# Retention's tiles from four pools, its roots stored by step, a shorter lag in attention, and row fetches issued five steps sooner

## The chip, the cores and the metric

The kernel runs on one core of a Trainium2 chip. The metric is the device time of one execution in microseconds. Before the change it is 1906.09 us, the median of three runs (1904.04 to 1906.96).

A core has a matrix engine (TensorE, PE in the profile; its weight loads are PEld), three engines for elementwise work (VectorE or DVE, ScalarE or ACT, GpSimd or POOL) and a synchronisation engine (SyncE or SP), which here issues most of the DMA transfers; ScalarE issues the weight streams. Each engine runs its instructions in order. Data lies in the main memory, in SBUF (128 partitions) and in PSUM, where TensorE writes its products.

## The reference

One layer of an encoder over 2048 positions and a model width of 1024, in float32:

```python
h = rms_norm(x, norm_gain)
q_a, k_a, v_a, g_a, q_r, k_r, v_r, g_r, m_a, m_r = split_columns(h @ w_in)
o_a = chunk_band_attention(q_a, k_a, v_a, rel_bias)     # 8 heads of 64, chunks of 64, 8 chunks to the left
branch_a = (o_a * silu(g_a)) @ w_out_attn
o_r = retention_chunkwise(rotary(q_r), rotary(k_r), v_r, gn_gain)   # 8 heads, keys of 64, values of 128
branch_r = (o_r * silu(g_r)) @ w_out_ret
mixed = sigmoid(m_a) * branch_a + sigmoid(m_r) * branch_r
out = rms_norm(x + mixed @ w_out, final_gain)
```

Retention is a product of queries and keys under a decay mask, times the values, plus a state that is carried from step to step. Its output is normalised for each head and position: the mean over the 128 values is taken away, and the rest is multiplied by the reciprocal root of its variance.

## The kernel before, in words

Most products are held to float32 accuracy by splitting an operand into a high and a low part and adding three products. The large projections run as Strassen products over two halves of the sequence (s = 0, 1), of two blocks of 512 positions each (b = 0 to 3).

The stages are p0 (projections of the first half), attention and retention of the first half, p1, attention and retention of the second half, and then the output products (ba, br, out) on 23 buffers. While attention and retention run, TensorE is filled up with products of the next projection: `fill(n)` (line 686) takes n steps of a stream that `dense` (line 627) yields, where a step is a quarter of a product, three matmuls of 512 columns. The order of all instructions on each engine is the order in which the program writes them. Work that has to wait for other work is put off with `later(n, fn)` (line 245): fn is written out n steps on. `put` (line 258) does that with a store.

SBUF tiles come from pools. A pool of n buffers gives a tile a buffer whose earlier tile is done with; the first instruction that writes the new tile waits until the last use of the old one is over, be it an engine's read or a store. `E` (line 114) takes tiles of 128 x 512 from the pool of the phase that is open. Retention's phase has 22 such buffers (`E_RET`, line 57).

Retention (line 1615) handles four pairs of heads (p) and, in each half, four steps of 256 positions (st). A step has two items (i), one for each head of the pair. For an item, `scores` (line 1671) multiplies keys and queries (tile sr in PSUM), VectorE multiplies that by the decay mask (sm<-sr,dm), ScalarE makes the high part (sh), and POOL the low part (sl). `output` (line 1745) multiplies the values by these parts and adds the state's share, in the PSUM bank o, of which there is one. `evacuate` (line 1762) copies o to the tile oz, squares it (o2) on ScalarE, stores oz two steps later (ors<-oz) and splits the squares (o2h, o2l). `sums`, at line 1790, sums the squares over the 128 values with a matmul against a matrix that has a column of ones: the row of the PSUM tile ssq that gets the sum is chosen by which 32 columns of the matrix `ohr` are taken. It uses 32 rows, half of them in each half of the sequence, and 512 columns.

Scores run two items ahead of outputs. The six loads of scored operands (kr<-krs twice, qr<-qrs four times; `load_scored`, line 1624) are issued two steps ahead, those of the values (kd, vr; `load_valued`, line 1646) one step ahead, and a mask (dm; `load_mask`, line 1667) some items ahead of its pair. All of them are written on SP's queue, as are the stores of the gates (mas, mrs) that the stream makes meanwhile.

After the last step of a half a chain of twelve VectorE operations (line 1844) turns ssq into reciprocal roots, and one store writes them to `rsscr` (rss<-rt). `finish_yr` (line 1240) reads a row of them for each head and block, much later. In the first half the loads of a later projection's operands (b_p<-in_w_in, line 1962) are written next.

Attention (line 1413) transposes its weights in groups (tp), splits them (pth on ScalarE, ptl on VectorE), and multiplies the values by them into the PSUM bank po (`weighted`, line 1525). A group's product is put off by `PV_LAG` = 3 slots, that of the first group by 2 more. A slot is one step of filling together with attention's own work. The bank po of the head before is read out (oa<-po) in the meantime. The first group only exists for blocks that have a block to their left.

While p0 runs, `second_half` (line 891) prepares the second half's rows: four pieces, each of four fetches of 128 x 4 x 128 (xs<-in_x), which ScalarE scales eight steps later by the reciprocal norms, TensorE transposes (pst<-ident,xs), and whose sums and differences are stored (cs<-xs, cs<-s).

Of the kernel before, what the change touches and what calls it, by code (L numbers as in the profile page):

```python
# [56 lines left out]
E_RET = 22  # L57
# [12 lines left out]
ONE = 31  # L70
# [3 lines left out]
def hybrid_kernel(  # L74
# [118 lines left out]
    rsscr = [D(f"rss_{s}", [32, B]) for s in range(2)]  # L193
# [697 lines left out]
    def second_half(at):  # L891
# [25 lines left out]
        def piece(k):  # L917
            tiles = {}

            def fetch(i, f):  # L920
                a = tiles[i, f] = E(f"xs_{k}_{i}_{f}", shape=(P, 4, P))
                rows = x[0, (2 + i) * B:(3 + i) * B, 512 * f + k * P:512 * f + (k + 1) * P]
                dma(a, rows.rearrange("(t p) c -> p t c", p=P))
                later(8, lambda: scale(i, f))
# [44 lines left out]
            later(26, first)  # L969
            later(30, second)  # L970
            later(34, third)

        for k in range(4):
            later(at + 14 * 8 + 18 + 44 * k, lambda k=k: piece(k))
# [265 lines left out]
    def finish_yr(h, b, m, lead, hold=0):  # L1240

        a, u, r = (E(f"{n}_{h}_{b}") for n in ("yr", "yv", "rb"))
        dma(a, orscr[h // 2][b][h % 2])
        dma(u, urscr[h][b])
        dma(r, rsscr[b // 2][8 * b + h].rearrange("(o d) -> o d", o=1).broadcast_to([P, B]))

        def gated():
            dve.scalar_tensor_tensor(a, a, gn[:, h:h + 1], u, ALU.mult, ALU.mult)

        later(lead, gated)  # L1250
        later(lead + 2, lambda: (pool if m is None else dve).tensor_tensor(a, a, r, ALU.mult))
        if m is None:
            put(lead + 8, yrscr[h], a)
            return
        wh, wl = (w[:, h % 4, :] for w in R[m])
        at = max(lead + 5, hold - steps[0])
        later(at, lambda: act.copy(wh, a))
        later(at + 2, lambda: dve.tensor_tensor(wl, a, r32(wh), ALU.subtract))
# [154 lines left out]
    def attention(s, sbp, ps_wide):  # L1413
# [111 lines left out]
        def weighted(h, b, gr):  # L1525
# [43 lines left out]
            later(PV_LAG + (2 if gr == 0 else 0), product)  # L1569
# [45 lines left out]
    def retention(s, ps_ret):  # L1615
        RET_FILL = RET_FILLS[s]
        ssq = ps_ret.tile([32, 512], F32, tag="ssq", bufs=1, name="ssq")
# [48 lines left out]

        def load_mask(p, i):
            dms.setdefault(p, []).append(E(f"dm_{p}_{i}")[:, 0:T + P])
            dma(dms[p][i], dmask[2 * p + i])

        def scores(p, st, i):
# [11 lines left out]
            def masked():  # L1683
                sm = E(f"sm_{nm}")[:, 0:T + P]
                dve.tensor_tensor(sm, sp, dms[p][i], ALU.mult)
                later(2, lambda: high(sm))

            def high(sm):
                got.append(E(f"sh_{nm}", F32R)[:, 0:T + P])
# [3 lines left out]
            def low(sm):  # L1693
                got.append(E(f"sl_{nm}", F32R)[:, 0:T + P])
# [67 lines left out]
        def evacuate(p, st, ops):  # L1762
# [4 lines left out]
            def out_():  # L1767
                oz = E(f"oz_{nm}")
                o2 = E(f"o2_{nm}")
# [9 lines left out]
            def high(o2):  # L1779
                got.append(E(f"o2h_{nm}", F32R))  # L1780
# [3 lines left out]
            def low(o2):  # L1784
                got.append(E(f"o2l_{nm}", F32R))
# [4 lines left out]
            def sums():  # L1790
                sure(lambda: len(got) == 2)
                for i in range(2):
                    r = 8 * b + 2 * p + i
                    for n, t in enumerate(got):
                        pe.matmul(
                            ssq[:, un * T:(un + 1) * T], ohr[:, ONE - r:ONE - r + 32],
                            t[:, i * T:(i + 1) * T],
                            start=not begun[0], stop=(p == 3 and st == 4 * s + 3 and i == 1 and n == 1),
                            skip_group_check=True,
                        )  # L1800
                        begun[0] = True
# [41 lines left out]
        y, tmp, hv, var = (E(f"rt{n}")[0:32] for n in range(4))  # L1843
# [11 lines left out]
        chain.append(lambda: dma(rsscr[s], y))  # L1855
# [189 lines left out]
```

## Time and profile before

| | |
|---|---|
| median of three runs | 1906.09 us (1904.04 to 1906.96) |
| profiled execution | 1910.35 us |
| its span, first to last instruction | 1908.5 us |
| TensorE busy | 1866.8 us (98%) |
| VectorE, ScalarE, POOL busy | 1356.3, 932.0, 665.2 us |
| mean granted TensorE clock | 0.996 |
| retention, first half | about 572 to 735 us of the span |
| retention, second half | about 1322 to 1497 us |

Times in the profile are microseconds from the first instruction, unless marked as ns. A row names the engine, the operation, the tiles as output<-inputs (without their buffer numbers), the shapes and how many instructions it stands for. All instructions carry the line of one helper, L143, so tiles are told apart by their names. Brackets behind a row show how long the engine had been idle and what ended that. The granted clock is a share of full speed. TensorE's matmuls overlap, so the time that one costs in a stream is read from start to start.

### The profile page before, as it was taken

What the parts mean: (1) busy time and instruction counts of PE and PEld (TensorE: products, weight loads), DVE (VectorE), ACT (ScalarE), POOL (GpSimd) and SP (SyncE); (2) the same over time, 40 slices, a digit from 0 to 9 for tenths busy, and PEclk for the clock granted to TensorE, in tenths of its full rate; (3) what the DMA queues carried; (4) which work ended last, traced back from release to release, by engine and by line L of the source; (5) the groups of instructions that cost most, each with busy time, mean ns of one, the idle gap of its engine ahead of it and who ended that gap; (6) DMA issues with size and microseconds to landing.
All of it is one profiled execution on the core that took longest, in us unless ns stands there. A gap on an engine that the chain in (4) does not pass through costs nothing. (4 is left out here: it accounts for less than half of the span.)

```text
span 1908.5 us, 31057 instructions
## 1 busy us (share of the span) xinstructions
PE 1866.8 (98%) x10213; PEld 1606.6 (84%) x10213; DVE 1356.3 (71%) x2456; ACT 932.0 (49%) x1931; POOL 665.2 (35%) x583
## 2 busy tenths in 40 slices
PE   7999999999999999999999999999999999999998
PEld 6899889888888877899889888888888878888886
DVE  6879888667655657888798677765546766767665
ACT  7555554666654455443343666664445321223544
POOL 0102105455645552001105545554564000001775
PEclk9999999999999999999999999999999999999999
DMA  6586976666549997776776656545999999987673
GB/s 192 160 273 203 282 266 213 185 181 192 177 133 279 283 264 239 240 233 200 226 246 199 191 155 196 160 150 168 265 278 276 317 354 346 318 294 228 209 235 129
DMA packets 325553, 435.88 MB, mean 228 GB/s; under 512 B 29880, under 2 KB 191184, under 8 KB 325392
## 3 DMA queue, kind: packets, MB, share of 16 engines
q1 hardware_dynamic: 260096, 368.35, 60.3%
q10 hardware_dynamic: 65296, 65.55, 11.3%
q8 instruction: 81, 1.33, 0.3%
q14 instruction: 80, 0.66, 0.1%
HBM read 288.14 MB, written 145.64 MB: 227 GB/s over the span
## 5 line engine op out<-in xcount | busy, mean ns | idle before, releaser
L143 POOL TENSOR_SCALAR pr<-pr,rsum 128x640 f32<-128x640 f32 (+4 forms) x128 | 100.0, 782 | 197.0 <-DVE rsum L143 137.0
L143 DVE TENSOR_TENSOR ptl<-tp,pth 128x512 fp32r<-128x512 f32 (+1 forms) x168 | 100.3, 597 | 95.6 <-ACT pth L143 78.2
L143 ACT ACTIVATE pr<-pr,mn 128x640 f32<-128x640 f32 (+4 forms) x128 | 97.9, 765 | 121.9 <-DVE mn L143 98.9
L143 PE MATMUL ps_g_x<-r,wh_g 128*128 128x512 f32 x448 | 141.9, 398 | 1.0 <-ACT u_g L143 0.8
L143 PE MATMUL ps_g_z<-r,wh_g 128*128 128x512 f32 x448 | 142.0, 398 | 0.1
L143 POOL TENSOR_TENSOR l_vr<-vrt,h_vr 128x512 fp32r<-128x512 f32 x32 | 47.7, 1491 | 201.8 <-DMA qrs<-l_q 131.4
L143 POOL TENSOR_TENSOR t_out<-raw_out 128x512 f32<-128x512 f32 x7 | 14.1, 2009 | 262.5 <-DVE wl_out L143 262.5
L143 DVE CUSTOM_DVE_ANT_0 pr<-wide,bt 128x640 f32<-128x640 f32 (+4 forms) x128 | 93.7, 732 | 16.4 <-PE wide L143 13.4
L143 ACT CAST pth<-tp 128x512 fp32r<-128x512 f32 (+1 forms) x168 | 85.3, 508 | 40.1 <-PE tp L143 31.0
L143 PE MATMUL wide<-ka,qa 128*128 128x384 f32 (+1 forms) x448 | 94.9, 327 | 4.0 <-DVE mn L143 3.5
L143 DVE TENSOR_TENSOR sm<-sr,dm 128x384 f32<-128x384 f32 x64 | 35.6, 556 | 88.7 <-DMA dm<-in_dmask_dram 31.7
L143 PEld LDWEIGHTS tp<-ident,pr 128*128 128x128 f32 x560 | 71.7, 140 | 25.2 <-POOL pr L143 2.7
L143 PEld LDWEIGHTS ps_g_x<-r,wh_g 128*128 128x128 f32 x448 | 80.4, 190 | 14.6 <-ACT u_g L143 2.2
L143 POOL TENSOR_TENSOR sl<-sm,sh 128x384 fp32r<-128x384 f32 x64 | 69.3, 1082 | 66.9 <-ACT sh L143 49.4
L143 ACT CAST wh_p<-raw_p 128x512 fp32r<-128x512 f32 x111 | 68.0, 619 | 50.3 <-PE ps_p_y L143 18.3
L143 PEld LDWEIGHTS ps_g_z<-r,wh_g 128*128 128x128 f32 x448 | 80.5, 190 | 13.6 <-DVE c_g L143 0.5
L143 PE MATMUL tp<-ident,pr 128*128 128x128 f32 x560 | 89.5, 272 | 1.5 <-POOL pr L143 1.2
L143 PE MATMUL ps_g_x<-r,wl_g 128*128 128x512 f32 x224 | 88.8, 396 | 0.0
L143 PE MATMUL ps_g_z<-r,wl_g 128*128 128x512 f32 x224 | 88.6, 395 | 0.0
L143 POOL TENSOR_TENSOR wl_g<-t_g,wh_g 128x512 fp32r<-128x512 f32 x56 | 75.0, 1340 | 35.1 <-ACT wh_g L143 34.8
L143 DVE TENSOR_TENSOR wl_p<-raw_p,wh_p 128x512 fp32r<-128x512 f32 x111 | 79.5, 723 | 7.6 <-ACT wh_p L143 4.8
L143 POOL TENSOR_TENSOR t_g<-raw_g,t_g 128x512 f32<-128x512 f32 x56 | 73.5, 1313 | 28.5 <-issue 8.0
(927 smaller groups left out, 6016.0 us busy)
## 6 DMA issues: line engine op xcount, KB each, us to landing
raw_g<-in_w_in_dram ACTq DMA_DIRECT2D x56, 512.0 KB, 4.7
raw_p<-in_w_in_dram ACTq DMA_DIRECT2D x50, 512.0 KB, 5.9
qa<-qas SPq DMA_DIRECT2D x128, 128.0 KB, 3.4
qr<-qrs SPq DMA_DIRECT2D x128, 128.0 KB, 4.6
vr<-vrs SPq DMA_DIRECT2D x64, 256.0 KB, 5.5
ka<-kas SPq DMA_DIRECT2D x56, 256.0 KB, 4.3
va<-vas SPq DMA_DIRECT2D x40, 256.0 KB, 3.2
kds<-kdt_k SPq DMA_DIRECT2D x32, 256.0 KB, 4.8
```

The lines of the kernel that those rows point to most:

```text
L143: return tc.keep_in_program_order(op(*a, **k))
```

## The change

- Retention's tiles come from four pools instead of one of 22 buffers: 11 for loaded operands, 7 (of 384 columns) for sm, sh and sl, 4 for oz, o2, o2h and o2l, and 3 for masks.
- ssq has 16 rows, one for each pair of heads and step of the half. A row holds both heads' 256 positions, so two matmuls of 512 columns replace four of 256. The matrix `ohr` gets narrower. `rsscr` has 16 rows, and four stores write it, one for each step, in the order in which `finish_yr` reads. The filling behind the chain is as long as the chain, hence three steps longer.
- In attention's first half the first group's product is put off by one slot more than the others, instead of two; in the second half by two, as before.
- The fetches of the second half's rows are written five steps sooner. Scaling and all that follows stay at their steps.

```diff
--- before.py
+++ after.py
@@ -54,7 +54,9 @@
 CS = 6
 E_PROJ = 19
 E_ATT = 11
-E_RET = 22
+E_RET = 11
+D_RET = 7
+O_RET = 4
 E_MRG = 23
 PR_BUFS = 5
 ATT_FILLS = (1.0, 1.0)
@@ -67,7 +69,7 @@
 TR_LATER = 16
 YR_0 = (2, 10, 1)
 YR_1 = (102, 15, 2)
-ONE = 31
+ONE = 15
 
 
 @with_exitstack
@@ -190,7 +192,7 @@
     escr = D("escr", [HEADS, 511])
     bandscr = [D(f"band_{h}", [P, 256]) for h in range(HEADS)]
     stscr = [D(f"sts_{p}", [HD, 2 * DV]) for p in range(4)]
-    rsscr = [D(f"rss_{s}", [32, B]) for s in range(2)]
+    rsscr = [D(f"rss_{s}", [16, B]) for s in range(2)]
     skscr = [D(f"sks_{p}", [P, 2 * DV], F32R) for p in range(4)]
 
 
@@ -921,7 +923,7 @@
                 a = tiles[i, f] = E(f"xs_{k}_{i}_{f}", shape=(P, 4, P))
                 rows = x[0, (2 + i) * B:(3 + i) * B, 512 * f + k * P:512 * f + (k + 1) * P]
                 dma(a, rows.rearrange("(t p) c -> p t c", p=P))
-                later(8, lambda: scale(i, f))
+                later(13, lambda: scale(i, f))
 
             def scale(i, f):
                 a = tiles[i, f]
@@ -966,12 +968,12 @@
             later(3, lambda: fetch(1, 1))
             later(6, lambda: fetch(0, 0))
             later(10, lambda: fetch(0, 1))
-            later(26, first)
-            later(30, second)
-            later(34, third)
+            later(31, first)
+            later(35, second)
+            later(39, third)
 
         for k in range(4):
-            later(at + 14 * 8 + 18 + 44 * k, lambda k=k: piece(k))
+            later(at + 14 * 8 + 13 + 44 * k, lambda k=k: piece(k))
 
     def refill(m, k, src, lag):
 
@@ -1242,7 +1244,7 @@
         a, u, r = (E(f"{n}_{h}_{b}") for n in ("yr", "yv", "rb"))
         dma(a, orscr[h // 2][b][h % 2])
         dma(u, urscr[h][b])
-        dma(r, rsscr[b // 2][8 * b + h].rearrange("(o d) -> o d", o=1).broadcast_to([P, B]))
+        dma(r, rsscr[b // 2][8 * (b % 2) + h].rearrange("(o d) -> o d", o=1).broadcast_to([P, B]))
 
         def gated():
             dve.scalar_tensor_tensor(a, a, gn[:, h:h + 1], u, ALU.mult, ALU.mult)
@@ -1566,7 +1568,7 @@
 
             part("h")
             later(1, lambda: part("l"))
-            later(PV_LAG + (2 if gr == 0 else 0), product)
+            later(PV_LAG + (1 + s if gr == 0 else 0), product)
 
         def plan(b):
 
@@ -1614,7 +1616,7 @@
 
     def retention(s, ps_ret):
         RET_FILL = RET_FILLS[s]
-        ssq = ps_ret.tile([32, 512], F32, tag="ssq", bufs=1, name="ssq")
+        ssq = ps_ret.tile([16, 512], F32, tag="ssq", bufs=1, name="ssq")
         state = epool[0].tile([HD, 2, DV], F32, tag="state", bufs=1, name="state")
         sstks = {}
         todo = [(p, st) for p in range(4) for st in range(4 * s, 4 * s + 4)]
@@ -1664,8 +1666,15 @@
                 dma(r32(sstk).rearrange("p i c -> p (i c)"), r32(skscr[p]))
                 sstks[p, 4] = sstk
 
+        def D_(name, dt=F32):
+            return epool[0].tile([P, T + P], dt, tag="d", bufs=D_RET, name=name)
+
+        def O_(name, dt=F32):
+            return epool[0].tile([P, 512], dt, tag="o", bufs=O_RET, name=name)
+
         def load_mask(p, i):
-            dms.setdefault(p, []).append(E(f"dm_{p}_{i}")[:, 0:T + P])
+            t = epool[0].tile([P, T + P], F32, tag="m", bufs=3, name=f"dm_{p}_{i}")
+            dms.setdefault(p, []).append(t)
             dma(dms[p][i], dmask[2 * p + i])
 
         def scores(p, st, i):
@@ -1681,17 +1690,17 @@
             got = []
 
             def masked():
-                sm = E(f"sm_{nm}")[:, 0:T + P]
+                sm = D_(f"sm_{nm}")
                 dve.tensor_tensor(sm, sp, dms[p][i], ALU.mult)
                 later(2, lambda: high(sm))
 
             def high(sm):
-                got.append(E(f"sh_{nm}", F32R)[:, 0:T + P])
+                got.append(D_(f"sh_{nm}", F32R))
                 act.copy(got[0], sm)
                 later(2, lambda: low(sm))
 
             def low(sm):
-                got.append(E(f"sl_{nm}", F32R)[:, 0:T + P])
+                got.append(D_(f"sl_{nm}", F32R))
                 pool.tensor_tensor(got[1], sm, r32(got[0]), ALU.subtract)
 
             later(1, masked)
@@ -1765,8 +1774,8 @@
             got = []
 
             def out_():
-                oz = E(f"oz_{nm}")
-                o2 = E(f"o2_{nm}")
+                oz = O_(f"oz_{nm}")
+                o2 = O_(f"o2_{nm}")
                 act.copy(oz, ops)
                 act.activation(o2, ops, AF.Square)
                 put(
@@ -1777,28 +1786,25 @@
                 later(2, lambda: high(o2))
 
             def high(o2):
-                got.append(E(f"o2h_{nm}", F32R))
+                got.append(O_(f"o2h_{nm}", F32R))
                 act.copy(got[0], o2)
                 later(2, lambda: low(o2))
 
             def low(o2):
-                got.append(E(f"o2l_{nm}", F32R))
+                got.append(O_(f"o2l_{nm}", F32R))
                 pool.tensor_tensor(got[1], o2, r32(got[0]), ALU.subtract)
 
             later(1, out_)
 
             def sums():
                 sure(lambda: len(got) == 2)
-                for i in range(2):
-                    r = 8 * b + 2 * p + i
-                    for n, t in enumerate(got):
-                        pe.matmul(
-                            ssq[:, un * T:(un + 1) * T], ohr[:, ONE - r:ONE - r + 32],
-                            t[:, i * T:(i + 1) * T],
-                            start=not begun[0], stop=(p == 3 and st == 4 * s + 3 and i == 1 and n == 1),
-                            skip_group_check=True,
-                        )
-                        begun[0] = True
+                r = 4 * (st - 4 * s) + p
+                for n, t in enumerate(got):
+                    pe.matmul(
+                        ssq, ohr[:, ONE - r:ONE - r + 16], t, start=not begun[0],
+                        stop=(p == 3 and st == 4 * s + 3 and n == 1), skip_group_check=True,
+                    )
+                    begun[0] = True
 
             return sums
 
@@ -1840,7 +1846,7 @@
         fill(9)
         pend()
 
-        y, tmp, hv, var = (E(f"rt{n}")[0:32] for n in range(4))
+        y, tmp, hv, var = (E(f"rt{n}")[0:16] for n in range(4))
         chain = [
             lambda: dve.tensor_scalar(var, ssq, 1.0 / DV, GN_EPS, ALU.mult, ALU.add),
             lambda: dve.tensor_scalar(tmp.bitcast(I32), var.bitcast(I32), 1, None, ALU.logical_shift_right),
@@ -1852,7 +1858,9 @@
                 lambda: dve.tensor_tensor(tmp, tmp, y, ALU.mult),
                 lambda: dve.scalar_tensor_tensor(y, tmp, 1.5, y, ALU.add, ALU.mult),
             ]
-        chain.append(lambda: dma(rsscr[s], y))
+        dst = rsscr[s].rearrange("(b p i) (u t) -> b u p i t", b=2, p=4, u=2)
+        for n in range(4):
+            chain.append(lambda n=n: dma(dst[n // 2, n % 2], y[4 * n:4 * n + 4].rearrange("p (i t) -> p i t", i=2)))
         for n, fn in enumerate(chain):
             later(1 + n, fn)
         fill(len(chain))
```

## The prediction

> **What bounds the kernel now.** I read the profile's page first, then the busy time by stretches, then the waits of TensorE, then the engines that TensorE waits for.
>
> ```profile
> span 1908.5 us, 31057 instructions
> PE 1866.8 (98%) x10213; PEld 1606.6 (84%) x10213; DVE 1356.3 (71%) x2456; ACT 932.0 (49%) x1931; POOL 665.2 (35%) x583
> ```
>
> TensorE bounds the kernel; 42 us of its span are idle, and an edit pays only as far as it shortens what TensorE does or waits for. The profiled execution took 1910.35 us in all, 1.85 us around its span. That is 0.2% above the median of 1906.09 us: the sum is made against 1910.35 us, and its share is carried over to the median. The stretches with retention's two halves come first, then three short ones behind waits (columns: stretch, its length, busy time of PE, PEld, DVE, ACT, POOL with instructions, granted TensorE clock, DMA share, GB/s):
>
> ```profile
> 572.00:735.00 163.00, 156.84 (x909) 134.15 (x908) 90.68 (x174) 78.90 (x155) 92.75 (x78) 0.99 0.87 256
> 1322.00:1497.00 175.00, 170.53 (x975) 146.61 (x974) 91.80 (x173) 85.91 (x167) 91.10 (x75) 0.99 0.92 279
> 701.90:706.30 4.40, 4.31 (x14) 3.56 (x15) 1.21 (x2) 0.21 (x1) 3.14 (x3) 0.61 0.88 274
> 1472.60:1478.00 5.40, 5.40 (x23) 4.53 (x24) 4.80 (x11) 3.16 (x7) 2.58 (x2) 0.68 0.83 232
> ...
> 278.20:283.00 4.80, 4.80 (x24) 4.34 (x25) 2.06 (x4) 4.80 (x15) 0.00 (x0) 0.65 0.62 208
> ```
>
> In retention TensorE idles 6.2 and 4.5 us, far above its average, and the DMA engines are 0.87 and 0.92 busy. Behind three waits the granted clock fell to 0.61, 0.68 and 0.65 over 4.4, 5.4 and 4.8 us: 0.39 x 4.4 = 1.7, 0.32 x 5.4 = 1.7 and 0.35 x 4.8 = 1.7 us of work lost each, beside the wait. Which waits these are, from TensorE's waits (total us, times, longest):
>
> ```profile
> PE o L143 <- ACT o L143: 2.9, 3, 1.5
> PE sr L143 <- DMA qr<-qrs: 2.5, 2, 1.7
> PE ssq L143 <- POOL o2l L143: 2.4, 3, 1.1
> PE pst L143 <- ACT xs L143: 2.2, 1, 2.2
> ...
> PE o L143 <- POOL sl L143: 0.4, 1, 0.4
> ```
>
> The slow stretches follow the longest waits of rows one, two and four (1.5, 1.7 and 2.2 us); no wait of 1.1 us or less has one. So a wait from about 1.5 us up costs 1.7 us more than it lasts.
>
> The Trainium skill (TensorE: Matmul & The Clock Gate, Part 1) puts this otherwise: the array is throttled after an idle window of about 3.4 us, free-running. By that figure a wait of 1.5 to 2.2 us would lower nothing; the rows above show it lowered three times out of three, so the measurement decides. If the slow stretches had another cause and stayed, the gain below would be smaller by the two of them that I count, 3.4 us, and the time 1899.7 us; after three cases of three I give that 0.05, inside the forecast's own chance and range.
>
> **The change, part by part.**
>
> *Retention's tiles from four pools.* Twenty-two mixed buffers become 11 for loads, 7 for masked scores and their parts, 4 for a step's output and squares, 3 for masks. What mixing costs now:
>
> ```profile
> ACT sh L143 <- DMA ors<-oz: 43.8, 13, 5.6
> ...
> POOL sl L143 <- DMA ors<-oz: 6.0, 2, 3.5
> ```
>
> The cast of a score part (sh) gets a buffer that the output copy oz held, and stands until the store of oz has landed. ScalarE works in order, so what is queued behind stands too: casts for the projections, and the copy and the square that empty the PSUM bank o. Here is one instance, ScalarE and then TensorE:
>
> ```profile
> 669.56 0.51 ACT L143 CAST sh<-sm 128x384 fp32r<-128x384 f32 x1 [5.62 <-DMA ors<-oz]
> ...
> 672.15 0.50 PE L143 MATMUL o<-qr,sstk 128*128 128x256 f32 x2 [0.91 <-ACT o L143]
> ```
>
> With own pools sh can never wait for a store. Seven buffers cover it: when sm of an item is allocated, the two parts of the item before last have just been consumed, and at most five stay live. So the o waits can go: 2.9 us, and 1.7 us of slow clock behind the 1.5 us one, 4.6 us. But the store is now waited for elsewhere. With four buffers for four tiles a step, oz or the square of one step takes the buffer whose store was issued in the step before:
>
> ```profile
> L143 SPq DMA_DIRECT2D ors<-oz x32: 366/384/711, 588.0 to 1489.6; - x32
> ...
> DMA to landing us min/median/max: 2.3/5.4/8.0
> ```
>
> A step is 163 / 16 = 10.2 us, or 175 / 16 = 10.9 us; issued two deferral steps after the copy, a store lands 7 to 10 us after it, mostly before the next copy and sometimes 1 to 2 us after. That wait stands directly ahead of the bank's release, while today's sits one position earlier and is longer. I take **-4.0 us** (bounds -4.6 and 0). The waits for POOL (ssq and the sl of o), 2.8 us, hang on ScalarE only in part, as POOL's own tile sums also wait for weights: **-1.4 us** (bounds -2.8 and 0).
>
> For the loads, 11 buffers are near today's share. Nine are live when the scored operands of two steps ahead are loaded (three of each of the two sets for the next step, and qr1 and two vr of this one). The third tile, qr1, must wait until this step's second output has run; today the six transfers of such a set already spread:
>
> ```profile
> 691.33 1.80 SPq L143 DMA_DIRECT2D kr<-krs  x2
> 693.76 2.39 SPq L143 DMA_DIRECT2D qr<-qrs  x4
> ```
>
> That is 691.33 to 696.15, 4.8 us, about the distance of two outputs (half a step, 5.1 us). Behind a held qr1 queue on SP the next kd and vr, the store of oz, gate stores and a mask. The late qr of 701.99 us (1.7 us and 1.7 us of slow clock, and 0.8 us elsewhere in that row) was such a set, so I take 0 here, with bounds -4.2 (it goes) and +17 (five more like it, 3.4 us each).
>
> *Roots by step.* The four sums of 256 columns become two of 512. Starts of TensorE show both spacings:
>
> ```profile
> 591.18 0.62 PE L143 MATMUL ps_g_z<-r,wh_g 128*128 128x512 f32 x2
> 591.63 0.39 PE L143 MATMUL ps_g_z<-r,wl_g 128*128 128x512 f32 x1
> 591.86 0.28 PE L143 MATMUL ssq<-o2h,ohr 128*32 128x256 f32 x1
> ...
> 592.33 0.40 PE L143 MATMUL o<-qr,sstk 128*128 128x256 f32 x2
> ```
>
> Four narrow ones take 592.33 - 591.86 = 0.47 us, two wide ones 2 x 0.68 / 3 = 0.453 us; 0.017 x 32 steps = **-0.5 us**. The chain on VectorE keeps its free size of 512, hence its time. Its one store becomes four, and the fill behind it is three steps longer, so in the first half the loads for the next projection (b_p) come later:
>
> ```profile
> 746.95 0.32 SPq L143 DMA_DIRECT2D rss<-rt  x1
> 747.79 2.17 SPq L143 DMA_DIRECT2D b_p<-in_w_in_dram  x4
> ...
> 753.50 0.60 ACT L143 CAST wh_p<-b_p 128x512 fp32r<-128x512 f32 x1
> ...
> 758.72 0.62 PE L143 MATMUL ps_p_x<-r,wh_p 128*128 128x512 f32 x2
> ```
>
> Three issues more are about 1.3 us with their spacing, and up to four r loads may go ahead, 1.9 us: 1.3 to 3.2 us later. The cast would start by 756.7, its other half follows as today 1.8 us behind (by 758.5 or so), and the matmuls are due at 758.72: covered, barely. I take 0 (bounds 0 and +2). In the second half nobody needs the roots for a long time.
>
> *Fetches five steps sooner.* The scaling stays where it was. Today the last piece is late:
>
> ```profile
> 270.90 0.32 SPq L143 DMA_DIRECT2D kds<-kdt_k  x1
> ...
> 273.38 2.17 SPq L143 DMA_DIRECT2D xs<-in_x_dram  x3
> ...
> 269.53 0.62 ACT L143 CAST wh_p<-t_p 128x512 fp32r<-128x512 f32 x1 [1.43 <-PE ps_p_w L143]
> 277.73 1.57 ACT L143 ACTIVATE xs<-xs,rs 128x128 f32<-128x128 f32 x5 [7.57 <-DMA xs<-in_x_dram]
> ...
> 275.71 0.28 PE L143 MATMUL ps_p_x<-wh_p,r 128*128 128x256 f32 x1
> 278.18 1.20 PE L143 MATMUL pst<-ident,xs 128*128 128x128 f32 x4 [2.19 <-ACT xs L143]
> ```
>
> A step is three wide matmuls, 0.68 us, so five are 3.4 us of emission. Passing only the five stores of 270.90 to 273.33 brings the fetch 2.5 us forward, and the scaling to 275.2, ready for TensorE at 275.6, where it comes free at 276.0. So the 2.2 us go and their 1.7 us of slow clock: **-3.9 us**. The stores that are passed land some 2.5 us later, and they are read only in later phases. Each piece holds four buffers of 19 for 3.4 us longer; if that stalls SP, a stall like this one moves elsewhere (bounds -3.9 and +3.9).
>
> *Attention's lag.* In the first half the first group's product is one slot sooner:
>
> ```profile
> 364.82 0.55 DVE L143 TENSOR_TENSOR ptl<-tp,pth 128x384 fp32r<-128x384 f32 x1
> ...
> 365.36 0.66 DVE L143 TENSOR_TENSOR oa<-po,oa 64x512 f32<-64x512 f32 x1
> ...
> 366.56 0.60 PE L143 MATMUL tp<-ident,pr 128*128 128x128 f32 x4
> ...
> 367.45 0.22 PE L143 MATMUL po<-pth,va 128*128 128x128 f32 x1
> ```
>
> It moves from 367.45 to ahead of the transposes at 366.56; its operand is there at 365.37 and the bank po is read out at 366.02, 0.5 us before. 0 us; with that cover gone, eight units at 0.3 us make +2.4; earlier free buffers bound the gain at -1.
>
> **Sum:** -4.0 - 1.4 - 0.5 - 3.9 = -9.8 us, 1910.35 to 1900.55, a share of 0.51%; of 1906.09 that leaves **1896.3 us**.
>
> **The rivals.** *The wait only moves:* the store of oz now holds the square in as many steps as it held sh (13 of 32), and TensorE waits as before. For it: landings up to 8.0 us. Against: the wait comes later in the step. Then only roots and fetch pay, -4.4 us: 1901.7 us. *Loads behind a held qr1 (slower):* place, SP at the third scored tile, until the second output has run. Landing takes this long (min/median/max):
>
> ```profile
> DMA to landing us min/median/max: 2.5/4.6/7.5
> ```
>
> qr1, issued after the second output of a step, is due one step later, 10.2 us minus the scores and its own two issues, some 8 us; at 7.5 us it just holds, and a second such delay on SP breaks it. Each break costs 3.4 us; against 9.8 us of gain three decide, and five make +7.2 us: 1913.3 us. Against it: today's sets are no sooner. *All retention waits go*, the qr ones too (4.2), with the rest of o and POOL (0.6 and 1.4): -16.0 us, 1890.1 us. A change without effect would need the pools to give the same waits and the fetch to stay late; SP's order shows no sign of it.
>
> **How the numbers follow.** Forecast 0.53, wait moves 0.20, loads held 0.14, all go 0.13. The forecast's own range is 1892 to 1902 us; with the rivals, and a tenth left out at each end, 1889 to 1909 us. Within 0.2% (3.8 us, about what a measurement of this kernel can tell from no change) means 1902.3 to 1909.9. The moved wait lies on that edge and is split evenly, 0.10 each; of held loads 0.11 are slower and 0.03 the same; the forecast gives 0.50 faster and 0.03 the same. Faster 0.10 + 0.50 + 0.13 = 0.73, same 0.16, slower 0.11.
>
> **What would show it.** No sh waits for ors<-oz; if oz or the square does, its total says how much moved, and the o waits of TensorE whether it mattered. pst waits for nothing, and the clock near 280 us is full. 64 ssq matmuls, 512 wide. The qr waits tell the held loads: more than two, or one above 1.5 us per half, and the forecast is wrong there. A wait ahead of ps_p_x near 757 us shows late b_p loads.

## The result, and the profile after

The changed kernel takes 1909.96 us (median of 21 runs, 1904.99 to 1916.40), the kernel before 1906.09 us (21 runs, 1901.63 to 1911.41). The ratio is 1.0022, with a 95% interval of 1.0012 to 1.0032: slower by some 4 us. The profiled execution of the changed kernel took 1916.40 us and is the slowest of its 21; that of the kernel before lay 4.3 us above its median. So both profiles hold more waiting than a median execution, and sizes are taken from many runs below.

The page of the changed kernel, and its waits of TensorE (total us, times, longest):

```profile
span 1914.5 us, 30827 instructions
PE 1870.0 (98%) x10149; PEld 1602.3 (84%) x10149; DVE 1361.2 (71%) x2456; ACT 933.8 (49%) x1931; POOL 665.7 (35%) x583
```

```profile
PE sr L145 <- DMA qr<-qrs: 5.8, 4, 2.4
PE kv L145 <- DMA vr<-vrs: 4.5, 5, 2.5
...
PE ps_g_x L145 <- ACT u_g L145: 1.4, 2, 0.8
PE ssq L145 <- POOL o2l L145: 1.4, 2, 1.0
PE ps_p_x L145 <- ACT u_p L145: 1.3, 1, 1.3
...
PE ps_ba_(0, 1)_18618 L145 <- DVE ga L1277: 0.9, 1, 0.9
...
PE pst L145 <- ACT xs L145: 0.7, 2, 0.5
```

The waits for ScalarE at the bank o, 2.9 us before, are gone, and the one ahead of pst has shrunk from 2.2 to 0.7 us. In their place TensorE waits 10.3 us for qr and vr (3.6 us before), a new wait stands ahead of ps_p_x, and the products ba wait 2.0 us for ga in all (1.3 before). ScalarE's longest waits in retention are now for VectorE and TensorE:

```profile
ACT sh L145 <- DVE sm L145: 35.6, 26, 4.0
ACT oz L145 <- PE o L145: 33.3, 20, 5.0
```

The 43.8 us for which sh waited for stores of oz have no row any more. As the first rival had it, a part moved: oz, the square o2 (written o in the row, as numbers are left out) and o2h wait 8.8 us for such stores in the two halves. TensorE waits at the bank o no more all the same. The rows of the first half, then that of the second:

```profile
ACT oz L145 <- DMA ors<-oz: 1.9, 1, 1.9
ACT o2h L145 <- DMA ors<-oz: 1.8, 1, 1.8
ACT o L145 <- DMA ors<-oz: 1.1, 1, 1.1
...
ACT o L145 <- DMA ors<-oz: 4.0, 4, 1.9
```

Retention still gained nothing, and the slow clock is behind the load waits now (stretches as in the prediction):

```profile
572.00:735.00 163.00, 156.63 (x873) 132.13 (x874) 94.06 (x174) 79.70 (x154) 90.97 (x77) 0.98 0.86 255
1322.00:1497.00 175.00, 168.45 (x928) 142.27 (x927) 89.78 (x167) 86.12 (x166) 90.36 (x75) 0.98 0.92 273
...
599.00:603.00 4.00, 4.00 (x15) 3.18 (x15) 1.38 (x2) 0.77 (x2) 3.80 (x4) 0.64 0.96 300
```

Behind the first half SP writes the roots and then loads b_p; SP's queue there, and what ScalarE and TensorE wait for:

```profile
746.59 0.75 SPq L145 DMA_DIRECT2D rss<-rt  x1
747.44 0.38 SPq L145 DMA_DIRECT2D mrs<-g  x1
747.87 0.67 SPq L145 DMA_DIRECT2D rss<-rt  x1
748.63 1.81 SPq L145 DMA_DIRECT2D r<-cs  x4
750.50 1.31 SPq L145 DMA_DIRECT2D rss<-rt  x2
751.85 2.09 SPq L145 DMA_DIRECT2D b_p<-in_w_in_dram  x4
...
755.45 0.62 ACT L145 CAST wh_p<-b_p 128x512 fp32r<-128x512 f32 x1 [2.21 <-DMA b_p<-in_w_in_dram]
...
757.12 0.73 PE L145 MATMUL ps_p_x<-r,wh_p 128*128 128x512 f32 x2 [1.32 <-ACT u_p L145]
```

b_p is issued at 751.85 us, 4.1 us later than before, and TensorE stands 1.32 us. The starts of the same instructions in both traces give the stages:

| from the start of ... to that of ... | before, us | after, us |
|---|---|---|
| the first instruction, the first transpose of attention's first half | 353.91 | 353.54 |
| that, the first score of retention's first half | 219.33 | 218.46 |
| that, the last sum of squares of the half | 161.92 | 162.69 |
| that, the first transpose of attention's second half ("behind the first half") | 329.24 | 331.82 |
| that, the first score of retention's second half | 259.60 | 259.21 |
| that, the last sum of squares | 172.68 | 176.10 |
| that, the first product br ("stage ba") | 76.42 | 77.57 |
| that, the last matmul | 326.43 | 326.43 |

Each part had its promise in another stage, so the parts were run one by one.

### The profile page after: what moved, and what is told of

Read it like the earlier page. It is cut to its first block, busy times and chain, and to the rows that moved or that the text cites. A ratio compares the mean times of both kernels' runs of the same rounds, so it can differ in the third digit from the quotient of the medians.

```text
span 1914.5 us, 30827 instructions
## 1 busy us (share of the span) xinstructions
PE 1870.0 (98%) x10149; PEld 1602.3 (84%) x10149; DVE 1361.2 (71%) x2456; ACT 933.8 (49%) x1931; POOL 665.7 (35%) x583
## 5 line engine op out<-in xcount | busy, mean ns | idle before, releaser
L145 DVE CUSTOM_DVE_ANT_0 pr<-wide,bt 128x640 f32<-128x640 f32 (+4 forms) x128 | 93.7, 732 | 16.7 <-PE wide L145 13.7
```

Source lines behind the costliest of these rows:

```text
L145: return tc.keep_in_program_order(op(*a, **k))
```

## The experiments

All ratios are against the kernel before, run beside each on the same chip, with 95% intervals in brackets; 0.001 is 1.9 us.

**Parts alone.** The fetches five steps sooner, nothing else (the hunks at 921 and 966 of the diff):

```diff
-                later(8, lambda: scale(i, f))
+                later(13, lambda: scale(i, f))
...
-            later(at + 14 * 8 + 18 + 44 * k, lambda k=k: piece(k))
+            later(at + 14 * 8 + 13 + 44 * k, lambda k=k: piece(k))
```

> Only the fetches five steps sooner, everything else as before. In the two profiles the last transposes of the rows came 1.5 us sooner after the change and the granted clock between 276 and 283 us rose from 0.76 to 1.00, but 1.2 of the 1.5 us were lost again before attention began. Theory one (the wait really went): 1.5 to 3.5 us faster than before, and the transposes' wait of 2.2 us is 0.7 us or less. Theory two (what is gained is given back when the stage ends late anyway, because the four buffers held longer make other loads later): no difference within 0.7 us, and the row of attention's first transposes starts at the same time as before.

1902.19 us, ratio 0.9984 (0.9973 to 0.9995). The waits of TensorE from 250 to 345 us, and beside them those of a kernel without the sooner fetches (roots_fill_as_before, below) with its stretch from 276 to 283 us:

```profile
PE ps_g_x L143 <- ACT u_g L143: 0.8, 1, 0.8
PE pst L143 <- ACT xs L143: 0.5, 1, 0.5
```

```profile
PE pst L143 <- ACT xs L143: 2.0, 1, 2.0
...
276.00:283.00 7.00, 5.51 (x42) 5.05 (x43) 4.20 (x8) 5.97 (x17) 0.00 (x0) 1.00 0.69 208
```

The wait goes from 1.5 to 2.2 us in the six profiles without sooner fetches to 0.5 to 1.3 us in the twelve with them, but a wait for u_g comes in at 322 us, 0.7 to 0.8 us with the sooner fetches and 0.0 to 0.2 us without: of 1.5 us some 0.8 are given back. The last transpose starts 1.4 us sooner on the average of the twelve than of the six (286.2 and 287.6 us), attention's first transpose only 0.3 us (352.0 and 352.3). So the time met theory one and the stage looks like theory two; where the rest of this run's 3.0 us (0.9 to 5.1) comes from is not shown. And the slow clock that the prediction charged to this wait is no fixed price: the wait of 2.0 us above left the clock at 1.00.

The roots by step alone, as in the change (the hunks at 67, 190, 1242, 1614, 1777, 1840 and 1852, without the pools), then the same with one store that writes the 16 rows as they stand, read back in two pieces of 256:

```diff
-        for n in range(4):
-            chain.append(lambda n=n: dma(dst[n // 2, n % 2], y[4 * n:4 * n + 4].rearrange("p (i t) -> p i t", i=2)))
+        chain.append(lambda: dma(rsscr[s], y))
...
+        rows = rsscr[b // 2].rearrange("(c u p) (i t) -> c p i u t", c=2, u=2, i=2)[b % 2, h // 2, h % 2]
+        dma(r.rearrange("p (u t) -> p u t", u=2), rows.rearrange("(o u) t -> o u t", o=1).broadcast_to([P, 2, T]))
```

> Only the roots by step: 16 rows of sums, 512 columns wide, four stores, the filling behind the chain three steps longer. Prediction: 0.5 us faster, tail free. Theory now: the later b_p loads cost about 1.5 to 2.6 us behind the first half, so 1 to 2 us slower than before, with a wait of TensorE of more than 1 us ahead of ps_p_x near 757 us. If the tail is not the cause, the time is 0.5 us below before and that wait is missing.

> Roots by step as in the change, but one store writes all 16 rows as they stand and the filling behind the chain is as long as before; finish_yr reads a row in two pieces. Theory one (the stores and the longer filling cost time): 0 to 0.7 us faster than before, 1.5 to 2.5 us faster than the same with four stores. Theory two (the wide sums themselves cost time, by putting off what stands behind them): as slow as with four stores.

Four stores: 1910.35 us, 1.0027 (1.0015 to 1.0038). This part alone is as slow as the whole change, 5 us where 1 to 2 were expected. One store: 1915.24 us, 1.0053 (1.0039 to 1.0067), a miss of both theories, since the reads in two pieces have a price of their own. VectorE's waits in stage ba say which:

```profile
DVE yr L1252 <- DMA rb<-rss: 11.7, 7, 3.0
```

The kernel before waits 3.9 us there. The pieces land 7.1 us after issue, whole rows 4.9 to 6.0 us in the profiles that have them (medians), and stage ba takes 82.3 us. So this form tells nothing of the sums, nor does the next one:

> The four pools on top of the roots by step with one store, no other part of the change. It is to be read against the run with one store alone: the difference is what the pools do. Prediction: 5.4 us faster than that. Theory one (loads are held back by the third scored tile): 3 to 5 us slower than that run, most of it in the second half of retention (3.5 us between its first and last score), and the waits of SP's queue for TensorE's o matmuls are 8 us or more per half against 2.5 and 4.9 us before. Theory two (the pools are neutral or better, and the profiled run of the changed kernel was merely an unlucky one): within 1 us of that run or faster.

1915.97 us, 1.0059 (1.0042 to 1.0076), within 1 us of the run without the pools, but with the same slow reads. To set the pools apart cleanly, narrow sums and one store were kept, in 16 rows instead of 32:

```diff
-                    r = 8 * b + 2 * p + i
+                    r = 8 * (b % 2) + 2 * p + i
-        ssq = ps_ret.tile([32, 512], F32, tag="ssq", bufs=1, name="ssq")
+        ssq = ps_ret.tile([16, 512], F32, tag="ssq", bufs=1, name="ssq")
```

> The four pools alone: sums of 256 columns and one store as before (in 16 rows instead of 32, so that the tiles fit in). Prediction: 5.4 us faster than before (the o waits and part of the POOL waits go). Theory one (what ScalarE no longer waits for is given back by loads behind a held third tile): 0 to 4 us slower than before; SP's waits for TensorE's o matmuls reach 8 us or more per half, and TensorE waits more for qr and vr. Theory two (the slowdown is all in the roots): 3 to 6 us faster than before, although SP waits as long.

> Lag and fetches only, on the one pool of 22 and sums of 256 columns. The fetches alone were 3.4 us faster than before. Prediction for the lag: nothing (bounds -1 and +2.4), so 3.4 us faster than before again. If the lag pays, 4 to 5 us faster; if it costs, 1 to 2.5 us faster and TensorE waits for ptl or oa in the first half of attention.

> Pools and fetches, attention's lag as before, narrow sums, one store. Parts alone: pools 2.0 us faster, fetches 3.4 us faster, fetches with lag 0.3 us faster, all three 2.8 us faster. If the lag costs 2 to 3 us: 4.5 to 6 us faster than before, 1900 to 1901 us. If the lag pays or is nothing (attention's first half was 1.2 us shorter with it in the profiles): 2 to 3 us faster, no better than with the lag.

> The change without the roots by step: pools, lag and fetches, sums of 256 columns, one store of 16 rows. The sum of the parts so far: the changed kernel is 3.9 us slower than before and the roots alone 4.8 us slower, so about 1 us faster than before if the parts add up; 5 us or more faster if it is the roots within the new pools that spoil them; no faster than before if the roots cost less beside the pools.

| parts on this base | median, us | ratio |
|---|---|---|
| pools | 1903.81 | 0.9990 (0.9979 to 1.0001) |
| lag, fetches | 1905.53 | 0.9995 (0.9984 to 1.0006) |
| pools, fetches | 1903.25 | 0.9990 (0.9979 to 1.0002) |
| pools, lag, fetches: all but the roots | 1902.99 | 0.9981 (0.9969 to 0.9993) |

The pools alone gain 2 us, less than theory two and no loss as in theory one, and beside the lag the fetches' 3 us are only 1. Single differences are near what these runs can tell. A least-squares fit of four parts, weighted by the intervals, to the eight kernels that are made of them (the changed one, these four, the fetches alone, the roots with 16 and with 13 steps of filling) gives roots +5.3, fetches -2.0, pools -1.0, lag +0.9 us, each with a standard error of 0.7 to 1.0; single kernels lie up to 1.7 us off it. The lag's sign isn't settled by that; its own stage, attention's first half, took 217.3 to 218.7 us in the ten profiles with the shorter lag and 219.3 to 220.2 in the eight without.

**Why the roots cost.** Four forms, with three diffs in this order: the roots alone, all four stores written out in one step with 13 steps of filling; three such stores that nobody reads, ahead of the one plain store of the version without the roots by step; the changed kernel with two stores of eight rows. The fourth is the changed kernel with the one plain store of the diff further up and the reads left as they are, so that the rows are mixed up and only its time is of use.

```diff
+        def stores():
+            for n in range(4):
+                dma(dst[n // 2, n % 2], y[4 * n:4 * n + 4].rearrange("p (i t) -> p i t", i=2))
+        chain.append(stores)
```

```diff
-        chain.append(lambda: dma(rsscr[s], y))
+        dst = spare[s].rearrange("(b p i) (u t) -> b u p i t", b=2, p=4, u=2)
+        def stores():
+            for n in range(3):
+                dma(dst[n // 2, n % 2], y[4 * n:4 * n + 4].rearrange("p (i t) -> p i t", i=2))
+            dma(rsscr[s], y)
+        chain.append(stores)
```

```diff
-                r = 4 * (st - 4 * s) + p
+                r = 8 * (st % 2) + 4 * (st // 2 - 2 * s) + p
...
+            for n in range(2):
+                dma(dst[n], y[8 * n:8 * n + 8].rearrange("p (i t) -> p i t", i=2))
```

> The roots by step with four stores, as in the change, but all four are written out in one step, so that the filling behind the chain is as long as before (13 steps, not 16); the rest as before the change. The roots alone, with 16 steps, were 4.8 us slower than before. Theory one (three more steps of filling put b_p off, and shift what stands behind it): 0 to 2 us slower than before, and the row of attention's second transposes begins 1.5 to 2 us sooner after the last sum than with 16 steps (331.7 us there, 329.2 us before). Theory two (the four stores and the reads of them cost it): 4 us slower or more.

> The change without the roots by step (pools, lag, fetches, narrow sums), but ahead of the one store of the roots three more stores of the changed kernel's shape (four rows, each in two pieces of 256) go to a spare buffer that nobody reads. Theory one (the four stores are the cost: each takes 0.63 us on SP's queue, against 0.32 us for one plain store, and what stands behind them comes 2.3 us later): 3 to 5 us slower than the same without them (1903.0 us); the first half's last sum to the second half's first transpose takes 331.5 us, not 329.4, and from the last sum to the first ps_br 77 us, not 74.3. Theory two (the wide sums are the cost): no slower than that run by more than 1 us.

> The changed kernel, but one store writes the 16 rows of roots as they stand, 13 steps of filling, and they are read as if they lay in the order of heads and blocks: the positions' roots are mixed up, everything else is computed. It shows what the wide sums are worth without the price of the store. Theory one (stores are the cost): 1902 to 1903 us, 0.5 us faster than with narrow sums, and 6 to 7 us faster than the changed kernel. Theory two (wide sums are the cost): within 2 us of the changed kernel, 1908 to 1911 us.

> The changed kernel with its 16 rows in another order (odd steps behind even ones), so that two stores of eight rows do what four of four rows did; written out in one step, 13 steps of filling. Theory one (the stores' time on SP): half of the cost goes, 2.5 to 3.5 us faster than the changed kernel, 1906 to 1907.5 us. If the cost hangs on the number of rows and pieces and not on the number of stores: as slow as the changed kernel, each store 1.2 us on SP. If the wide sums are the cost: as slow, too, but the stores short.

| kernel | ratio | behind the first half, us | stage ba, us |
|---|---|---|---|
| roots alone, four stores, 16 steps | 1.0027 (1.0015 to 1.0038) | 331.65 | 77.25 |
| roots alone, four stores, 13 steps | 1.0019 (1.0005 to 1.0033) | 331.68 | 77.92 |
| all but the roots | 0.9981 (0.9969 to 0.9993) | 329.43 | 74.29 |
| the same, three stores more | 1.0011 (1.0001 to 1.0021) | 331.56 | 75.99 |
| changed, one plain store, rows mixed | 0.9996 (0.9984 to 1.0008) | 329.38 | 74.83 |
| changed, two stores | 1.0001 (0.9992 to 1.0010) | 329.87 | 75.57 |
| changed | 1.0022 (1.0012 to 1.0032) | 331.82 | 77.57 |

Three stores that do nothing make the good version 0.0030 slower, 5.7 us; taking the four shaped stores out of the changed kernel takes 5.0 us away, and halving their number 4.0 us. The wide sums are not the cause, nor, as far as 1.0027 against 1.0019 can tell, are the three steps of filling. The rows of the stores: of the kernel before, of the roots with 13 steps, and the spare ones (shortest, median and longest ns on SP's queue):

```profile
L143 SPq DMA_DIRECT2D rss<-rt x2: 323/324/324, 746.9 to 1507.1; - x2
```

```profile
L143 SPq DMA_DIRECT2D rss<-rt x8: 608/631/757, 740.5 to 1506.9; - x8
```

```profile
L145 SPq DMA_DIRECT2D spare<-rt x6: 609/650/758, 742.9 to 1504.4; - x6
```

A store in pieces holds SP 0.63 to 0.65 us, a plain one 0.32. Behind the first half the delay reaches TensorE by different doors: at ps_p_x with 16 steps (1.1 us in the roots alone), and with three spare stores some 30 us later, in the waits from 735 to 800 us (a wait of 1.4 us stands there with 13 steps too, none in all but the roots):

```profile
PE ps_p_z L145 <- DVE wl_p L145: 1.3, 1, 1.3
```

TensorE's idle time in this stage is 3.1 to 3.4 us in the five profiles with four stores in a half (the three spare ones included) and 1.3 to 2.2 us in the other thirteen.

In stage ba the stretches of 80 us from the last sum on show the DMA engines fuller without the four stores, first all but the roots, then the changed kernel:

```profile
1487.00:1567.00 80.00, 80.00 (x355) 66.23 (x354) 59.08 (x94) 20.86 (x35) 0.00 (x0) 1.00 0.97 342
```

```profile
1502.00:1582.00 80.00, 77.95 (x340) 63.26 (x340) 57.69 (x91) 20.85 (x35) 0.00 (x0) 1.00 0.93 329
```

In the changed kernel TensorE stands 2.0 us of this stretch and waits for ga, none in the other; the kernel before, with its one plain store, stands 1.3 us there. VectorE makes ga, and what it waits for in this stretch is not the roots (rb: 0.2 us, against 1.8 us in all but the roots) but the gates yv (4.8 against 2.3 us) and the casts of ba's weights (8.6 against 3.8 us); ScalarE, which makes these casts, waits 11.9 against 4.5 us for the loads raw_ba. SP issues these loads among and behind the stores. (With all stores in one step only yv is clearly later: VectorE waits 5.4 us for it in the roots with 13 steps and 4.0 us with the spare stores.) That a delay there is not caught up because the DMA engines are 0.97 busy is argued from this, not shown.

**Where the pools' gain went.** Waits in both retention halves together, from all profiles:

| kernels | TensorE for ScalarE at o, us | TensorE for qr and vr, us | SP for TensorE's o, us |
|---|---|---|---|
| one pool of 22 (six) | 2.8 to 4.6, mean 3.6 | 1.4 to 3.7, mean 2.6 | 6.0 to 12.6 |
| four pools, 11 load buffers (nine) | 0.0 to 0.8 | 3.6 to 10.3, mean 5.5 | 15.2 to 25.4 |

What went at o, some 3.4 us, came back as 2.9 us of late qr and vr. SP's column is where the held third tile of the prediction would show; the row for it in each half, of the kernel before and of the changed one:

```profile
SPq L143 <- PE o L143: 2.5, 6, 0.5
...
SPq L143 <- PE o L143: 4.9, 9, 0.9
```

```profile
SPq L145 <- PE o L145: 8.7, 9, 3.1
...
SPq L145 <- PE o L145: 12.2, 13, 3.2
```

To tell whether that is the cause, all but the roots was run with 12 load buffers, its cost taken from the other pools, with a control; and with an own pool for oz alone beside 20 mixed buffers.

```diff
-E_RET = 11
-D_RET = 7
+E_RET = 12
+D_RET = 6
...
-            t = epool[0].tile([P, T + P], F32, tag="m", bufs=3, name=f"dm_{p}_{i}")
+            t = epool[0].tile([P, T + P], F32, tag="m", bufs=2, name=f"dm_{p}_{i}")
```

```diff
-E_RET = 22
+E_RET = 20
+O_RET = 2
...
-                oz = E(f"oz_{nm}")
+                oz = O_(f"oz_{nm}")
```

> Control for the next one: the change without the roots by step (pools, lag, fetches, narrow sums, one store; 2.8 us faster than before), with 6 buffers instead of 7 for masked scores and 2 instead of 3 for masks, and 11 for loads as in the change. At most five masked tiles stay live, so nothing new should wait for the 6; a mask may come later. 0 to 2 us slower than with 7 and 3. SP's waits for TensorE's o matmuls stay at 6 and 9 us or more per half, TensorE's for qr and vr at 4 us or more in all.

> As the control, with 12 load buffers instead of 11, so that the third scored tile has a buffer before the step's second output has run. Theory one (held loads eat the pools' gain): SP's waits for TensorE's o matmuls fall below half (under 8 us in both halves, single ones under 1 us), TensorE's waits for qr and vr fall by 2 us or more, and the time is 2 to 4 us below the control. Theory two (the DMA engines are the limit, 0.87 to 0.92 busy, and the order of loads does not matter): SP waits less, but qr and vr are as late and the time is within 1 us of the control.

> Lag, fetches, narrow sums and one store (0.3 us faster than before), with two buffers for oz alone and 20 mixed ones for everything else in retention: loads are not held by a count of their own, and no cast can wait for a store of oz. Theory one: TensorE's waits for ScalarE at the bank o (3.5 and 1.1 us with one pool) and SP's longer waits are both away; qr and vr as with one pool (1.5 us); 3 to 5 us faster than before, 1901 to 1903 us. Theory two (whatever waits less on ScalarE is late in the loads): within 1 us of lag and fetches alone, with qr and vr waits of 4 us or more.

| kernel | median, us | ratio | qr and vr, us | SP for o, us |
|---|---|---|---|---|
| 11 loads, 6, 2 masks (control) | 1900.25 | 0.9970 (0.9958 to 0.9982) | 5.2 | 17.9 |
| 12 loads, 6, 2 masks | 1898.22 | 0.9960 (0.9946 to 0.9973) | 3.2 | 5.9 |
| own pool for oz | 1900.35 | 0.9975 (0.9964 to 0.9986) | 4.8 | 5.6 |

The waits of TensorE with 12 buffers, and with the own pool for oz:

```profile
PE sr L145 <- DMA qr<-qrs: 2.3, 1, 2.3
...
PE kv L145 <- DMA vr<-vrs: 0.9, 3, 0.4
```

```profile
PE sr L144 <- DMA qr<-qrs: 2.7, 4, 1.2
PE kv L144 <- DMA vr<-vrs: 2.1, 6, 0.5
```

With the twelfth buffer SP's waits fall to a third and qr and vr come 2 us sooner, as the held tile would have it; the time falls by 2.0 us, but the two intervals overlap. The own pool for oz speaks against the held tile as the only cause: SP waits for o less than with one pool there, and qr and vr are late all the same. Its time is that of theory one, its late loads are those of theory two. In the changed kernel's profile, too, what SP stood for ahead of the longest wait for qr was a load of raw_g (4.9 us between 585 and 597 us), a wait that all kernels have. How much of the late loads is the held tile and how much the full queue therefore stays open. The control was to be 0 to 2 us slower than with 7 and 3 buffers (0.9981) and came out faster, within overlapping intervals. The version with 12 loads beats both kernels.

Last, the changed kernel as it is, with those 12, 6 and 2 buffers:

> The changed kernel, roots by step and four stores and all, with 12 load buffers, 6 for masked scores and 2 for masks. The same without the roots was 7.8 us faster than before (0.9960 of its time, 0.9946 to 0.9973). If the four stores have a price of their own, 4 to 6 us of that are gone: 0.998 to 0.999 of the time before, with 331.5 us from the first half's last sum to the second half's first transpose (329.5 us without) and more than 76 us from the last sum to the first ps_br (75.2 us without). If their price was in part that of held loads, 0.9965 to 0.9975, with at most half of that in these two places.

1902.60 us, 0.9992 (0.9978 to 1.0006). The waits for qr and vr are down to 1.1 us, retention's halves take 155.3 and 168.2 us, and yet it is 0.0032, 6.1 us, slower than without the roots by step: 332.5 us behind the first half (329.5 without), 81.4 us in stage ba (75.2), with these waits there:

```profile
PE ps_ba_(1, 0)_18549 L145 <- DVE ga L1277: 2.2, 1, 2.2
PE ps_ba_(1, 0)_18351 L145 <- DVE ga L1277: 0.9, 1, 0.9
PE ps_ba_(0, 1)_18423 L145 <- DVE ga L1277: 0.5, 1, 0.5
```

In this execution the granted clock also fell to 0.50 for 3.4 us behind the wait of 2.2 us and behind one of 1.9 us ahead of ps_p_x, 1.7 us of work each, so the two stages are longer than the stores' waits alone. The four stores keep their price beside 12 load buffers.

## Why the prediction was wrong

Forecast -9.8 us, measured +3.9: neither the direction nor the range held. Of the 13.7 us between them the fit puts 5.8 on the roots, 4.4 on the pools, 1.9 on the fetches and 0.9 on the lag, and leaves 0.7. By its steps:

- *Roots by step, -0.5 and a tail of 0 (bounds 0 and +2).* The step that failed. It measured +5.3 us in the fit, 5.7 with spare stores, 6.1 beside 12 load buffers. Two readings were wrong. "Three issues more are about 1.3 us": the price was that of the plain store in the one row at hand (0.32 us), while the new ones have another shape and hold SP twice as long; four take 2.8 us, so b_p was 2.5 us later for that alone, and the cover called "barely" there was used up (in the changed kernel r loads went ahead too, 4.1 us in all). The prediction's own sign of this, a wait ahead of ps_p_x near 757 us, came. And "in the second half nobody needs the roots for a long time": nobody waits long for them, but the first read of them (rb) is issued 3 us behind the store in the kernel before, and the loads that share SP's queue shift with the stores. Stage ba is 1.7 to 3.6 us longer in the three kernels with the four stores and 11 or 22 buffers and in the one with the spare stores than in all but the roots, and 6.3 us longer beside 12 load buffers, where a slow clock adds 1.7; the kernel before lies 2.1 us above all but the roots as well. The sums themselves behaved as told: 64 instructions, 512 wide.
- *Pools, -4.0 for ScalarE.* Right in mechanism and nearly in size: sh waits for no store, the 8.8 us that moved to oz, o2 and o2h did no harm at the bank, and the waits at o fell from 3.6 to 0.2 us on the average. *Loads, 0 (bounds -4.2 and +17).* The term was mis-sized: waits for qr and vr grew by 2.9 us. "Today's sets are no sooner" compared one set with the whole; with the new pools SP stands for o twice as long on the average. *POOL, -1.4.* The wait of ssq was 2.4 us in the profile before and 1.4 in the changed kernel's, but 0.4 to 1.3 us in the other five profiles with one pool and 1.4 to 1.6 us in all nine with four: no gain is shown. Net for the pools: -1.0 ± 0.7 us instead of -5.4.
- *Fetches, -3.9.* Right in sign, half the size: -2.0 in the fit, -3.0 alone. The wait did shrink, but 0.8 us come back at u_g, the starts of attention show 0.3 us, and the 1.7 us of slow clock stood behind this wait in only two of the six profiles without sooner fetches.
- *Lag, 0 (bounds -1 and +2.4).* Its stage became 1.6 us shorter, a little outside the bound; the whole shows nothing that can be told from zero.
- *"A wait from about 1.5 us up costs 1.7 us more."* Three of three in one profile. In the 18 profiles of this case TensorE was idle for 1.5 us or more 31 times after the first 100 us, and behind 14 of these the granted clock fell; a wait of 2.29 us left it at 1.00 (roots and 12 load buffers, 1328 us), one of 1.51 us did not (kernel before, 1473 us). The price was right where it fell due: the clock stands at 0.50 for 3.41 us, 1.7 us of work. When it falls due can be read from the times. All its falls and rises in a trace lie on one grid with cells of 3.413 us: in the kernel before it falls at 279.65, 702.91 and 1474.32 us, 124 and 226 cells apart. Of the cells at full clock all ten with 1.85 us or more of idle time were followed by a slow cell, six of 21 with 1.39 to 1.84 us, and none with less. So a wait that lies across the edge of two cells can go free, and two short ones can add up (1.2 and 0.9 us near 1465 us with the rows mixed). The Trainium skill (TensorE: Matmul & The Clock Gate, Part 1) tells of a free-running window; that a wait of one length is caught in some cases and not in others agrees with it, while its length of about 3.4 us is more than any of the 14 waits lasted.
- *The rivals.* The side was that of "loads behind a held qr1 (slower)", 1913.3 us, but not its mechanism: late loads, held or queued, took back part of one gain, and what made the kernel slower are the stores, which no rival named.

## What to carry to other kernels

Price a moved or split DMA by a row of its own shape, or by a wide bound where there is none, and ask for each place where it is issued what is queued behind it: here some 2.5 us more on the issuing queue came back as 2.1 to 2.4 us behind one half and 1.7 us or more in the stage whose DMA engines were 0.97 busy. A buffer count that frees one engine can hold the queue that feeds another, so count the live tiles at the moment of issue and try one more for the loads. And read a single profile's waits as one draw: the clock behind a wait of one length differed between profiles.

## What was not expected of the hardware

- A store whose rows go out in two pieces each took 0.61 to 0.76 us of SP's queue, with four rows and, in the run with two stores, with eight (0.70 to 0.80); a plain store of 16 or 32 rows took 0.32. The time hangs on the shape, hardly on the number of rows; whether it is the two pieces or the other order in memory is not told apart.
- The broadcast read of a row in two pieces of 256 landed 7.1 and 7.3 us after issue (medians of two profiles), that of a whole row 4.9 to 6.0 us; stage ba took 82.3 and 81.8 us with the pieces, 76.4 us in the kernel before.
- The granted clock fell behind 14 of 31 waits of 1.5 us or more; what counts is the idle time within one cell of a grid of 3.413 us, from 1.39 us in some cases, from 1.85 us in all.
